# One bank and one copy for the convolution's last rows, and the second up unit's weight sums ahead of its operand sums

## The chip, the cores and the metric

The kernel runs on one core of a Trainium2 chip. The metric is the device time of one execution in microseconds (us). The text uses the profile's names for the engines: PE is TensorE, DVE is VectorE, ACT is ScalarE, SP is the engine whose queue issues the DMAs. The program holds a list of instructions for each engine, and an engine goes through its list in order.

## What the kernel computes

One step of an encoder with one layer runs over 1024 prompt frames and 64 sample frames of width 1024 (T = 1088 columns). Two parts matter here. The first is the convolution module, whose last 30 inputs of either group are outputs of their own:

```python
u = a * jax.nn.sigmoid(g)
ext = jnp.concatenate([hist, u], axis=1)          # 30 rows of history, then the frames
y = depthwise_conv(ext, w, width=31) + bias       # 256 channels
yn = layer_norm(y) * ln_g + ln_b
return jax.nn.silu(yn), ext[:, -30:]              # conv output, and conv_p or conv_s
```

The second is the MLP at the end, `x + square(relu(rmsnorm(x) @ w_up)) @ w_down`, with 4096 hidden columns. Between them lie three attention mixers, the output projection `w_out` and an attention over 256 memory tokens.

## The kernel before

All big products are made of single-precision numbers split into a high and a low part (`split`, lines 168 to 171): ACT writes the high part, DVE subtracts it from the source and writes the low part. A product then takes three matmuls, high by high, high by low and low by high.

**What sets the order.** The order on each engine is made when the program is built. A planner plays the program through on a clock of its own, and gives each engine, whenever it is free, the ready instruction with the lowest priority number. The number counts up with the program text (`tc.cur_priority`); the text adds to it or sets it in a few places. A tile of a pool has a fixed number of buffers for each tag, and an instruction that first writes a tile can run only when a buffer of that tag is free.

**The mixer stage.** Four lanes (projections, attention, convolution, HGRN) are written as generators and interleaved; each has its own range of numbers, in the order projections, attention, HGRN, convolution, then the matmuls of the projections, and last everything behind the mixers (`PR_END`). The convolution (`lane_conv`, lines 758 to 836) works in three pieces of the time axis; both halves of the 256 channels (`ct`) have a tile `ext` of inputs and a tile `y` of sums. The 31 taps are 62 instructions on DVE for a piece (lines 788 to 794), a chain for each `ct`. In the last piece they are followed in the text by the last 30 columns: two transposes on PE into a PSUM tile `pco`, a copy by DVE into `cvo` (line 804) and a DMA, first for the prompt, then for the sample. PSUM tag `cv` has one buffer, so the second pair of transposes waits for the first copy. After them come the means and variances (`pme`, `pva`), the normalization, and the DMA of the result into `mix_d`. `cvo` takes its buffer from tag `c0` (one buffer, also used by `sg` and `rs`); tag `nat` of pool `wk` (two buffers) holds transposed keys and values on their way out, last those of the memory (`mnat`, line 402).

**The first products behind the mixers.** `dense_add(0, w_out, ...)` (line 1104) multiplies `w_out` by the mixers' outputs of the first 512 columns; its matmuls write `pa`. For each block of weights the low part `wl` is made by DVE.

**The up projection.** The hidden columns are made in 16 units of 256 (line 1367). Unit 0 is a plain product. Units 1 to 15 are Strassen-like: seven products of half size instead of eight. For this the operand is turned once into sums (`forms`, line 1302): for each of four `k`, `T1` and `T2` and `T3` and `T4` are made in place from the normalized columns and then split. The names of the operands are `B11`, `T1`, `B21`, `T2`, `B22`, `T3`, `T4`. For each unit the weights are turned into sums too (`sums`, lines 1328 to 1333, four additions of 128x512 that write into the loaded tiles `r1` and `r2`), and split into `S2`, `S1`, `S3`, `S4`, `A22`. The products of unit 1 come in the order `W` (first half of `pa` by `B11`), `W` (second half by `B21`, after ACT has copied the first result), `Y = S4 B22`, `Z = S2 T2`, `X = S1 T1`, then into the same PSUM tile `Z` again `S3 T3` and `A22 T4`, each time after DVE has added what was there to an output tile (`plus`, line 1344). Both weight tiles of a unit (`pa`, `pb`) come from tags `wh` and `wl`, which have two buffers; unit 1 gets them when unit 0 has used its own (`ws`). The second group's columns are normalized by `second` (line 1291), which runs 600 numbers late beside the end of the product before.

Of the kernel before, what the change touches and what calls it, by code (L numbers as in the profile page):

```python
# [8 lines left out]
F32 = mybir.dt.float32  # L9
# [8 lines left out]
P = 128  # L18
# [6 lines left out]
G = 256  # L25
# [27 lines left out]
def kernel(ctx: ExitStack, tc: tile.TileContext, *args):  # L53
    nc = tc.nc
# [18 lines left out]
    def act(out, in_, func, **kw):  # L73
        nc.scalar.activation(out=out, in_=in_, func=func, **kw)  # L74

    V, Q = nc.vector, nc.gpsimd
# [4 lines left out]
    ident = const.tile([P, P], F32, name="ident")  # L81
# [28 lines left out]
    for m in LEVELS[1:]:  # L110
        nb = 64 // m
        f = const.tile([P, nb], F32, name=f"lf{m}", tag="lvlf", bufs=1)
# [56 lines left out]
    def split(hi, lo, src):  # L169
        act(hi, src, AF.Copy)  # L170
        V.tensor_tensor(out=lo, in0=src, in1=hi.bitcast(F32), op=ALU.subtract)  # L171
# [5 lines left out]
    def fetch_w(src, r0, kt, c0, cols=P):  # L177
        raw = wp.tile([P, KD, P], F32, name="wr", tag="wr")[:, :kt, :cols]
        nc.sync.dma_start(out=raw, in_=src[r0:r0 + kt * P, c0:c0 + cols].rearrange("(k p) c -> p k c", p=P))
        return raw  # L180
# [43 lines left out]
    def pair(which):  # L224
        return [pools[which].tile([P, 576], F32R, name="ap", tag="ap") for _ in range(2)]
# [16 lines left out]
    wk = mx.enter_context(tc.tile_pool(name="wk", bufs=2))  # L242
    rb = wk.tile([P, T], F32, name="rb", tag="rb", bufs=1)
    with ExitStack() as pa:
# [6 lines left out]
        for i, (t0, n) in enumerate(TT):  # L251
# [3 lines left out]
            if i in (3, 6):  # L255
                c = (C_SK, C_SV)[i // 3 - 1]
# [43 lines left out]
    ps_cv = mx.enter_context(tc.tile_pool(name="ps_cv", bufs=1, space=PSUM))  # L300
# [169 lines left out]
    def halves(t):  # L470
        return t[:, :PAST], t[:, PAST:]
# [266 lines left out]
    HW = CW - 1  # L738
    CN = 376
    CE = SP - 2 * CN + HW + SS  # L740

    def ct_(name, tag, n=CN):
        return hc.tile([P, n], F32, name=name, tag=tag)
# [6 lines left out]
    ps = ps_cv.tile([P, 4, 64], F32, name="pcw", tag="cv")  # L750
# [7 lines left out]
    def lane_conv():  # L758
        tails = [None, None]
        for t0, np_ in ((0, CN), (CN, CN), (2 * CN, SP - 2 * CN)):  # L760
            last = t0 + np_ == SP
            n, nt = (CE, np_ + SS) if last else (np_, np_)
            ys, exts = [], []
# [32 lines left out]
                if j % 3 == 2:  # L796
                    yield 0.3 + n / 150.0
            if last:
                for at, dst in ((np_, conv_p), (CE, conv_s)):
                    ps = ps_cv.tile([P, G], F32, name="pco", tag="cv")  # L800
                    for ct in range(2):
                        nc.tensor.transpose(ps[:HW, ct * P:(ct + 1) * P], exts[ct][:, at:at + HW], ident)
                    ot = ct_("cvo", "c0")
                    V.tensor_copy(out=ot[:HW, :G], in_=ps[:HW])
                    nc.sync.dma_start(out=dst[0, 0], in_=ot[:HW, :G])
            rs = ct_("rs", "c0").rearrange("p (j n) -> p j n", j=2)
            sqs = [ct_(f"sq{ct}", f"ce{ct}", CN + HW) for ct in range(2)]
            for p0, pn in ((0, n // 2), (n // 2, n - n // 2)):
# [197 lines left out]
    class Lane:  # L1006
# [3 lines left out]
        def ready(self):  # L1010
            return self.need is None or self.need in done

    lanes = [Lane(lane_projections(), P_COST, PR_PROJ), Lane(lane_attention(), 1.0, PR_ATT),
             Lane(lane_conv(), 1.0, PR_CONV), Lane(lane_hgrn(), 1.0, PR_HGRN)]
    while lanes:
        ln = min((x for x in lanes if x.ready()), key=lambda x: x.t)
# [38 lines left out]
    def unit(tag, dt=F32):  # L1055
        return units[tag].tile([P, 576], dt, name=tag, tag=tag)

    xw = [[unit("xt") for k in range(KD)] for g in range(2)]
# [202 lines left out]
    def bank():  # L1261
        return psm.tile([P, 512], F32, name="pw", tag="w", bufs=2)

    def banks():
        return psm.tile([P, 2, 512], F32, name="pz", tag="z", bufs=3)
# [4 lines left out]
    def mul(ps, w, b, start, cols):  # L1270

        for k, (bh, bl) in enumerate(b):
            last = k == len(b) - 1
            mm(ps, w[0][:, k], bh[:, cols], start and k == 0, False, skip_group_check=not start)
            mm(ps, w[0][:, k], bl[:, cols], False, False, skip_group_check=not start)
            mm(ps, w[1][:, k], bh[:, cols], False, last, skip_group_check=not start)

    def mul2(ps, w, b, start, n=N2):
        mul(ps[:, 0, :HN], w, b, start, slice(0, HN))
        mul(ps[:, 1, :n - HN], w, b, start, slice(HN, n))  # L1280
# [21 lines left out]
    def forms(k):  # L1302

        (h11, h12), (h21, h22) = ((xw[0][i], xw[1][i]) for i in (k, k + 4))
        V.tensor_tensor(out=h11[:, :N1], in0=h12[:, :N1], in1=h11[:, :N1], op=ALU.subtract)
        act(h11[:, N1:], h12[:, N1:], AF.Copy)
        split(*hb[T1][k], h11)
        V.tensor_tensor(out=h12, in0=h22, in1=h12, op=ALU.subtract)
        V.tensor_tensor(out=h22, in0=h22, in1=h11, op=ALU.subtract)
        split(*hb[T2][k], h22)  # L1310
        split(*hb[T3][k], h12)
        V.tensor_tensor(out=h21[:, :N1], in0=h21[:, :N1], in1=h22[:, :N1], op=ALU.subtract)
        split(hb[T4][k][0][:, :N1], hb[T4][k][1][:, :N1], h21[:, :N1])
# [9 lines left out]
    def wform(src):  # L1323
        pr = [unit("ap", F32R)[:, :4 * P].rearrange("p (k c) -> p k c", k=4) for _ in range(2)]
        split(*pr, src)
        return pr

    def sums(a11, a12, a21, a22, s1, eng):

        eng.tensor_tensor(out=s1, in0=a21, in1=a22, op=ALU.add)  # L1330
        eng.tensor_tensor(out=a21, in0=a11, in1=a21, op=ALU.subtract)
        eng.tensor_tensor(out=a11, in0=s1, in1=a11, op=ALU.subtract)
        eng.tensor_tensor(out=a12, in0=a12, in1=a11, op=ALU.subtract)

    def square(out, c, scale=None):

        if scale is None:
            act(out, c, AF.Relu)
        else:
            V.scalar_tensor_tensor(out=out, in0=c, scalar=0.0, in1=scale, op0=ALU.max, op1=ALU.mult)  # L1340
        act(out, out, AF.Square)

    def plus(out, a, b, eng=V):
        eng.tensor_tensor(out=out, in0=a, in1=b, op=ALU.add)  # L1344

    def store_hidden(i, tiles):
        for m, g, t in zip((0, 0, 1, 1), (0, 1, 0, 1), tiles):
            t0, n, _ = GR[g]
            nc.sync.dma_start(out=hid_d[2 * i + m][:, t0:t0 + n], in_=t[:, :n])
# [17 lines left out]
    for i in range(1, NU):  # L1367
        r1 = fetch_w(w_up, 0, KD, 2 * i * P)
        r2 = fetch_w(w_up, 0, KD, (2 * i + 1) * P)
        pa, pb = ([wp.tile([P, KD, P], F32R, name=nm, tag=nm) for nm in ("wh", "wl")] for _ in range(2))  # L1370
        split(*pa, r1)
        if i == 1:
            tc.cur_priority += 800
            for k in range(4):
                forms(k)
        s1 = fz.tile([P, 4, P], F32, name="s1", tag="s1", bufs=1)
        sums(r1[:, :4], r1[:, 4:], r2[:, :4], r2[:, 4:], s1, V)
        S2, S1 = wform(r1[:, :4]), wform(s1)
        S3 = wform(r2[:, :4])
        S4, A22 = [t[:, :4] for t in pb], [t[:, 4:] for t in pb]  # L1380
        split(*S4, r1[:, 4:])
        split(*A22, r2[:, 4:])
        t1 = t1s[i % 2]
        W, Z, X = bank(), banks(), banks()
        mul(W, [t[:, :4] for t in pa], hb[B11], True, slice(0, N1))
        act(t1[:, :N1], W, AF.Copy)
        c12, c22 = unit("ap"), unit("ap")
        if i == 1:

            mul(W, [t[:, 4:] for t in pa], hb[B21], False, slice(0, N1))  # L1390
            Y = banks()
            mul2(Y, S4, hb[B22], True)
            plus(halves(c12), halves(t1), Y[:, :, :HN])
        mul2(Z, S2, hb[T2], True)
        plus(halves(c12), halves(c12 if i == 1 else t1), Z[:, :, :HN])
        mul2(X, S1, hb[T1], True)
        plus(halves(c22), halves(t1), X[:, :, :HN])
        if i == 1:
            plus(halves(c12), halves(c12), X[:, :, :HN])
        else:  # L1400
            mul(W, [t[:, 4:] for t in pa], hb[B21], False, slice(0, N1))
        c11 = unit("xt")
        square(c11[:, :N1], W)
        mul2(Z, S3, hb[T3], False)
        plus(halves(c22), halves(c22), Z[:, :, :HN])
        square(c22, c22, q)
        if i > 1:
            mul2(X, S4, hb[B22], False)
            plus(halves(c12), halves(c12), X[:, :, :HN])
        square(c12, c12, q)  # L1410
        mul2(Z, A22, hb[T4], False, N1)
        c21 = unit("xt")
        plus(c21[:, :HN], t1[:, :HN], Z[:, 0, :HN])
        plus(c21[:, HN:N1], t1[:, HN:N1], Z[:, 1, :N1 - HN])
        square(c21[:, :N1], c21[:, :N1])
        store_hidden(i, (c11, c12, c21, c22))
# [63 lines left out]
    for c in range(NC):  # L1480
# [5 lines left out]
        if c < NC - 1:  # L1486
            for j in range(KD // 2):
                for m, w in enumerate(down_w(c, j, None)):
                    ps = bank()
                    mul(ps, w, [hid[k][0] for k in range(NF)], True, slice(0, N1))  # L1490
                    plus(xT[0][2 * j + m], xT[0][2 * j + m], ps)
                    ps = banks()
# [3 lines left out]
        else:  # L1496

            ws = []
            for j in range(KD // 2):
                dst = [[t[:, :NF * P].rearrange("p (k c) -> p k c", k=NF) for t in pair(1 - c % 2)] for m in range(2)]  # L1500
                ws += down_w(c, j, dst)
            for g, c0, n in ((0, 0, 512), (1, 0, 320), (1, 320, 256)):
                for m in range(KD):
                    ps = bank()[:, :n]
# [37 lines left out]
```

## Time and profile before

| | before |
|---|---|
| median of 3 runs | 1772.66 us (1772.01 to 1775.33) |
| the profiled execution | 1772.62 us, span 1770.6 us |
| PE busy | 1698.2 us, 96% of the span |
| DVE busy | 1174.6 us, 66% |
| ACT busy | 791.5 us, 45% |
| granted TensorE clock, mean | 0.987 |

The span runs from the first to the last instruction; 2.0 us of the execution lie around it. A clock of 1.00 is the level of 2.4 GHz and 0.50 that of 1.2 GHz. Successive DVE instructions overlap by some 0.09 us at their ends, so that one listed with 0.69 us takes 0.60 us of the engine's time from start to start.

### The profile page before, as it was taken

To read this page: it belongs to the slowest core of one execution; us is meant where nothing else is said; L and a number is where in the kernel's file an instruction comes from. 1 tells how busy PE (TensorE), PEld (TensorE's weight loads), DVE (VectorE), ACT (ScalarE), POOL (GpSimd) and SP (SyncE) were. 2 spreads that over 40 slices of the span, in tenths; PEclk is the share of its full clock that TensorE was granted. 3 is DMA by queue.
4 is the path that set the end of the run, shared out by engine and by line. 5 is a ranking of instruction groups with operands and counts; after the bars stand their busy time and mean duration, and the time that the engine had idled before them with its cause. 6 is when DMAs were issued, how large, how long until landed. Compare 5 with 4: busy or idle time off the path is not lost.

```text
span 1770.6 us, 29390 instructions
## 1 busy us (share of the span) xinstructions
PE 1698.2 (96%) x11379; PEld 1506.6 (85%) x11379; DVE 1174.6 (66%) x2231; ACT 791.5 (45%) x1614; POOL 93.6 (5%) x201
## 2 busy tenths in 40 slices
PE   6999999999999979999999989999999999999997
PEld 4987768788777768988899979999999999999987
DVE  6366789988986897668777795555555444444435
ACT  5266657647356755346456353343334212122213
POOL 3021201101020100000000000000000000000000
PEclk9999999999999989999999999999999999999999
DMA  8521322243237357222522323333335732332112
GB/s 255 144 76 44 111 78 84 80 113 88 63 99 215 101 155 233 81 88 68 158 78 72 118 91 107 99 99 103 101 100 194 272 98 87 98 99 73 36 36 102
DMA packets 233195, 194.70 MB, mean 110 GB/s; under 512 B 17502, under 2 KB 199711, under 8 KB 233055
## 3 DMA queue, kind: packets, MB, share of 16 engines
q1 hardware_dynamic: 232799, 192.80, 35.5%
q8 instruction: 90, 1.47, 0.4%
q14 instruction: 50, 0.41, 0.1%
q0 software_dynamic: 256, 0.01, 0.0%
HBM read 137.96 MB, written 53.72 MB: 108 GB/s over the span
## 4 chain that ended last, share of the span: by engine, by line
PE 78%; DVE 13%; ACT 4%; DMA 2%; issue 2%; POOL 0%; SPq 0%; DVEq 0%; POOLq 0%; ACTq 0%
PE pz L71 25%; PE pw L71 16%; PE pm L71 11%; PE pa L71 9%; PE pq L71 5%; PE z L71 2%; DVE y L794 2%; PE pmo L71 2%; PE pms L71 1%; PE po L71 1%; PE pt L517 1%; PE pv L71 1%; DVE hsc L933 1%; DVE sba L494 1%; DVE wl L171 1%
## 5 line engine op out<-in xcount | busy, mean ns | idle before, releaser
L74 ACT ACTIVATE wh<-wr 128x1024 fp32r<-128x1024 f32 (+1 forms) x179 | 161.5, 910 | 446.6 <-PE pz L71 193.8
L171 DVE TENSOR_TENSOR wl<-wr,wh 128x1024 fp32r<-128x1024 f32 (+1 forms) x179 | 184.5, 1037 | 68.8 <-ACT wh L74 67.6
L71 PE MATMUL pw<-ap,wh 128*128 128x512 f32 x720 | 223.4, 391 | 1.3 <-ACT t L74 0.7
L71 PE MATMUL pz<-ap,wh 128*128 128x288 f32 x988 | 198.3, 294 | 0.0
L71 PE MATMUL pa<-ap,wh 128*128 128x256 f32 (+2 forms) x768 | 187.1, 332 | 2.2 <-DVE xt L1119 2.2
L71 PE MATMUL pm<-hx,wh 128*128 128x512 f32 (+1 forms) x640 | 176.4, 364 | 1.9 <-ACT wh L74 1.7
L71 PEld LDWEIGHTS pz<-ap,wh 128*128 128x128 f32 x988 | 161.3, 188 | 4.7
L71 PE MATMUL pm<-ap,wh 128*128 128x256 f32 (+1 forms) x768 | 164.7, 308 | 0.0
L71 PEld LDWEIGHTS pw<-ap,wh 128*128 128x128 f32 x720 | 130.1, 188 | 24.1 <-ACT t L74 1.1
L71 PE MATMUL pz<-ap,wl 128*128 128x288 f32 x494 | 145.5, 294 | 0.0
L71 PEld LDWEIGHTS pa<-ap,wh 128*128 128x128 f32 x768 | 131.7, 190 | 12.6 <-DVE xt L1119 2.4
L71 PE MATMUL pw<-ap,wl 128*128 128x512 f32 x360 | 140.4, 390 | 0.0
L71 PE MATMUL pa<-ap,wl 128*128 128x512 f32 (+2 forms) x384 | 126.8, 331 | 1.1 <-DVE wl L171 1.1
L71 PEld LDWEIGHTS pm<-hx,wh 128*128 128x128 f32 x640 | 110.5, 192 | 20.3 <-ACT wh L74 2.5
L71 PEld LDWEIGHTS pm<-ap,wh 128*128 128x128 f32 x768 | 123.9, 191 | 4.2 <-issue 1.7
L1344 DVE TENSOR_TENSOR xt<-xt,pz 128x576 f32<-128x576 f32 x56 | 42.2, 754 | 113.8 <-PE pz L71 108.5
L71 PE MATMUL pm<-ap,wl 128*128 128x256 f32 (+1 forms) x384 | 114.2, 297 | 0.0
L71 PE MATMUL pm<-hx,wl 128*128 128x512 f32 (+1 forms) x320 | 112.9, 353 | 0.3 <-DVE wl L171 0.2
L794 DVE SCALAR_TENSOR_TENSOR y<-ext,cwT,y 128x376 f32<-128x376 f32 (+1 forms) x180 | 101.1, 609 | 0.3
L1344 DVE TENSOR_TENSOR xt<-xt,pw 128x512 f32<-128x512 f32 (+2 forms) x80 | 51.1, 639 | 69.6 <-PE pw L71 69.6
L71 PE MATMUL pq<-ap,wh 128*128 128x512 f32 (+2 forms) x384 | 93.1, 332 | 0.0
L71 PEld LDWEIGHTS pz<-ap,wl 128*128 128x128 f32 x494 | 92.7, 188 | 0.0
(380 smaller groups left out, 3580.7 us busy)
## 6 DMA issues: line engine op xcount, KB each, us to landing
wr<-in_w_up_dram SPq DMA_DIRECT2D x32, 512.0 KB, 4.0
wr<-in_w_down_dram SPq DMA_DIRECT2D x32, 512.0 KB, 3.5
wr<-in_w_in_dram SPq DMA_DIRECT2D x24, 512.0 KB, 4.3
hid_d<-ap SPq DMA_DIRECT2D x32, 288.0 KB, 2.5
aq<-hid_d SPq DMA_DIRECT2D x32, 288.0 KB, 3.2
wr<-in_w_out_dram SPq DMA_DIRECT2D x16, 512.0 KB, 3.5
wr<-in_w_mq_dram SPq DMA_DIRECT2D x16, 512.0 KB, 3.7
wr<-in_w_mo_dram SPq DMA_DIRECT2D x32, 256.0 KB, 2.7
```

Of the source, the lines that this page charges most:

```text
L71: nc.tensor.matmul(out, lhsT=lhsT, rhs=rhs, start=start, stop=stop, **kw)
L74: nc.scalar.activation(out=out, in_=in_, func=func, **kw)
L171: V.tensor_tensor(out=lo, in0=src, in1=hi.bitcast(F32), op=ALU.subtract)
L494: V.tensor_tensor_scan(out=v[:, ::-1], data0=z[:, n - 1:0:-1], data1=v[:, ::-1], initial=-NEG, op0=ALU.add, op1=ALU.subtract)
L517: nc.tensor.transpose(ps[:w, j - jb], p[:, j * P:j * P + w], ident)
L794: V.scalar_tensor_tensor(out=y, in0=ext[:, j:j + n], scalar=cwT[:, ct, j:j + 1], in1=y, op0=ALU.mult, op1=ALU.add)
L933: V.copy_predicated(sc[r, s_at:s_at + ng, :, r].rearrange("p g h (c w) -> p (g h) c w", w=2 * m)[:, :, :, m:], lvl[m][r, par * nb:(par + 1 ...
L1344: eng.tensor_tensor(out=out, in0=a, in1=b, op=ALU.add)
```

## The change

The last rows of the convolution, prompt and sample, are transposed into one PSUM tile of a bank; one copy takes both out into a buffer of tag `nat`, and two DMAs store the halves. `forms` is cut in two: `forms` makes `T1` and `T2`, and a new `forms2` makes `T3` and `T4`; the text of unit 1 now first has the weight sums and their splits and then the operand sums, `T1` and `T2` of all four `k` ahead of `T3` and `T4`. The 800 numbers that were added in front of the operand sums are still added in front of them, so that the weight sums of unit 1 no longer have them.

```diff
             if last:
-                for at, dst in ((np_, conv_p), (CE, conv_s)):
-                    ps = ps_cv.tile([P, G], F32, name="pco", tag="cv")
+                ps = ps_cv.tile([P, 2, G], F32, name="pco", tag="cv")
+                for o, at in enumerate((np_, CE)):
                     for ct in range(2):
-                        nc.tensor.transpose(ps[:HW, ct * P:(ct + 1) * P], exts[ct][:, at:at + HW], ident)
-                    ot = ct_("cvo", "c0")
-                    V.tensor_copy(out=ot[:HW, :G], in_=ps[:HW])
-                    nc.sync.dma_start(out=dst[0, 0], in_=ot[:HW, :G])
+                        nc.tensor.transpose(ps[:HW, o, ct * P:(ct + 1) * P], exts[ct][:, at:at + HW], ident)
+                ot = wk.tile([P, 512], F32, name="cvo", tag="nat").rearrange("p (o c) -> p o c", o=2)
+                V.tensor_copy(out=ot[:HW], in_=ps[:HW])
+                for o, dst in enumerate((conv_p, conv_s)):
+                    nc.sync.dma_start(out=dst[0, 0], in_=ot[:HW, o])
...
         split(*hb[T2][k], h22)
+
+    def forms2(k):
+
+        (h11, h12), (h21, h22) = ((xw[0][i], xw[1][i]) for i in (k, k + 4))
         split(*hb[T3][k], h12)
         V.tensor_tensor(out=h21[:, :N1], in0=h21[:, :N1], in1=h22[:, :N1], op=ALU.subtract)
         split(hb[T4][k][0][:, :N1], hb[T4][k][1][:, :N1], h21[:, :N1])
...
         split(*pa, r1)
-        if i == 1:
-            tc.cur_priority += 800
-            for k in range(4):
-                forms(k)
         s1 = fz.tile([P, 4, P], F32, name="s1", tag="s1", bufs=1)
         sums(r1[:, :4], r1[:, 4:], r2[:, :4], r2[:, 4:], s1, V)
...
         split(*A22, r2[:, 4:])
+        if i == 1:
+            tc.cur_priority += 800
+            for f in (forms, forms2):
+                for k in range(4):
+                    f(k)
```

## Rows read from the trace of the kernel before

**Rows 1.** The page: busy us (share of the span) xinstructions
```profile
PE 1698.2 (96%) x11379; PEld 1506.6 (85%) x11379; DVE 1174.6 (66%) x2231; ACT 791.5 (45%) x1614; POOL 93.6 (5%) x201
```
**Rows 2.** Waits of PE, 640 to 1100 us: total, times, longest
```profile
PE pco L802 <- DVE cvo L804: 8.6, 1, 8.6
PE pz L71 <- ACT wh L74: 5.8, 1, 5.8
...
PE pw L71 <- ACT t L74: 0.7, 1, 0.7
```
**Rows 3.** Stretches: length, busy PE PEld DVE ACT POOL, PEclk, DMA, GB/s
```profile
657.40:662.00 4.60, 4.58 (x12) 3.91 (x13) 3.23 (x5) 0.68 (x1) 0.00 (x0) 0.50 0.69 199
...
1058.30:1062.10 3.80, 3.74 (x14) 3.39 (x15) 1.70 (x3) 0.48 (x1) 0.00 (x0) 0.50 0.31 85
...
1026.80:1060.00 33.20, 26.68 (x153) 23.39 (x153) 33.09 (x55) 20.84 (x36) 0.00 (x0) 0.93 0.14 51
```
**Rows 4.** Timeline of PE, 595 to 662 us: start, us, what, [idle]
```profile
609.32 0.28 PE L802 MATMUL pco<-ident,ext 128*30 128x128 f32 x1
...
645.86 1.20 PE L71 MATMUL pa<-ap,wh 128*128 128x512 f32 x4
655.68 0.61 PE L802 MATMUL pco<-ident,ext 128*30 128x128 f32 x2 [8.62 <-DVE cvo L804]
657.42 0.80 PE L71 MATMUL pa<-ap,wl 128*128 128x512 f32 x1 [1.12 <-DVE wl L171]
```
**Rows 5.** Timeline of DVE, 643 to 660 us
```profile
644.01 11.32 DVE L794 SCALAR_TENSOR_TENSOR y<-ext,cwT,y 128x366 f32<-128x366 f32 x22
655.23 0.40 DVE L804 COPY cvo<-pco 30x256 f32<-30x256 f32 x1
655.56 0.67 DVE L171 TENSOR_TENSOR ap<-mix,ap 128x512 fp32r<-128x512 f32 x1
656.16 1.21 DVE L171 TENSOR_TENSOR wl<-wr,wh 128x1024 fp32r<-128x1024 f32 x1
```
**Rows 6.** Groups of instructions by form, DVE, the whole span
```profile
L310 DVE COPY aT<-pt 128x512 f32<-128x512 f32 x11 | 7.5, 686 | 0.2 <-PE pt L517 0.2
```
**Rows 7.** The chain that ended last: start, us, what
```profile
660.77 1.22 PE pme L71 x4
...
1033.63 12.47 PE pz L71 x94
...
1109.20 9.27 PE pz L71 x72
...
1121.25 6.36 PE pz L71 x48
```
**Rows 8.** Timeline of SP, 540 to 660 us: DMAs of `mnat`
```profile
613.83 0.45 SPq L402 DMA_DIRECT2D out_dram<-mnat  x1
...
644.55 0.39 SPq L402 DMA_DIRECT2D out_dram<-mnat  x1
```
**Rows 9.** Timeline of PE, 1051 to 1064 us
```profile
1052.14 0.39 PE L71 MATMUL pw<-ap,wl 128*128 128x512 f32 x1
1058.31 0.85 PE L71 MATMUL pz<-fz,wh 128*128 128x288 f32 x2 [5.78 <-ACT wh L74]
```
**Rows 10.** Timeline of DVE, 1005 to 1100 us
```profile
1040.91 1.22 DVE L171 TENSOR_TENSOR wl<-wr,wh 128x1024 fp32r<-128x1024 f32 x1
...
1051.29 0.68 DVE L1330 TENSOR_TENSOR s<-wr 128x512 f32<-128x512 f32 x1
...
1056.90 0.69 DVE L1333 TENSOR_TENSOR wr<-wr 128x512 f32<-128x512 f32 x1
...
1059.31 0.69 DVE L171 TENSOR_TENSOR ap<-wr,ap 128x512 fp32r<-128x512 f32 x1
1063.96 0.75 DVE L1344 TENSOR_TENSOR ap<-t,pz 128x576 f32<-128x576 f32 x1 [3.96 <-PE pz L71]
```
**Rows 11.** Timeline of ACT, 1038 to 1066 us
```profile
1039.62 1.06 ACT L74 ACTIVATE wh<-wr 128x1024 fp32r<-128x1024 f32 x1 [0.50 <-PE pz L71]
```

## The prediction

> **What bounds the kernel now.** The page's first part comes first: PE is busy for 96% of the span [rows 1], so little but PE's idle time and the stretches at its lower clock can be won. The view of waits, for PE alone, says where that idle time lies behind the mixers: one wait of 8.6 us in front of the transposes `pco`, one of 5.8 us in front of a product `pz`, and small ones, as 0.7 us at `pw` [rows 2]. The table of stretches shows what each of the two long waits leaves behind it: a stretch in which PE is busy throughout but at 0.50, the level of 1.2 GHz (657.4 to 662.0 and 1058.3 to 1062.1 us, [rows 3]). Both waits are what the two edits touch. Last come the timelines of PE and DVE around the waits, to see who is late, and who is late next.
>
> **Edit 1, the convolution's last rows.** In PE's list the second pair of transposes stands behind the first four `pa` products; those end at 647.1, the pair starts at 655.68 and waits for the first `cvo` copy [rows 4]. The first pair ran long before (609.32, [rows 4]). With one tile for all four, none needs a copy first, and I expect the second pair beside the first one. The wait at `pco` goes. What is late next stands two rows on: the next `pa` product waits for `wl` until 657.42 [rows 4], and DVE makes `wl` only behind 22 taps in a row, the copy and a low part `ap` [rows 5]. Nothing in the edit takes these off DVE, and the taps have lower numbers than all that follows the mixers. So PE idles nearly as long as before. Term by term:
> - The copy on this path now takes 512 columns for 256. Copies cost 0.40 us for 30x256 [rows 5] and 0.69 for 128x512 [rows 6]: `wl` is 0.29 us later, +0.3. The second copy, which goes, ran behind this `wl`, beside a busy PE: nothing.
> - The mean's four products `pme` need the last tap and the bank behind the copy. Before they ran in the middle of the `pa` products and cost the chain 1.22 us [rows 7]. Now they can run at 656, while PE waits for `wl`: -1.2, if the planner puts them ahead; 0 if not. I take -1.2, since their numbers are lower than those of `pa`.
> - Two transposes more at 597 to 610, 0.3 us each by [rows 4], in a list that meets the wait above anyway: 0; exposed they cost +0.6.
> - The stretch at 0.50 begins with the idle time and I keep it whole; if PE's work starts 1.4 us sooner, up to -0.7 (half of that).
>
> Sum of edit 1: -0.9 us. Its ends: +0.9 (both doubtful ones lost) and -1.9.
>
> **Edit 2, the second up unit.** Between 1026.8 and 1060.0 us DVE has no idle time (33.09 of 33.20 us, [rows 3]): it makes the operand sums and, last of all, the four weight sums and their splits, from 1051.29 to 1060.0 [rows 10]. PE starts the last product of `W` at 1052.14 [rows 9], is free at 1052.4 and needs `S4`, which needs all four sums; the fourth starts at 1056.90 [rows 10], and PE starts at 1058.31 [rows 9]. The work on DVE is the same after the change (9 instructions of 0.60 us from start to start, 5.4 us, go to the front); only its order changes. So I date each product by what DVE has finished when PE comes for it.
> - The third sum writes over `r1`, which the split of `pa` reads. That split starts on ACT at 1039.62 behind a PE product, as `wh` comes free [rows 11], and ends on DVE at 1042.1 [rows 10]. Sums three and four then end at 1043.3, `S2`, `S1`, `S3` at 1045.1. `S4` and `A22` need the second `wh` buffer, which unit 0 leaves with its last product at 1046.1 [rows 7]; with two results of unit 0 in between I put `S4` at 1047.5. PE wants it at 1052.4, so the wait of 5.8 us is gone.
> - PE then takes 3.18 us each for `Y`, `Z`, `X` and `S3 T3` (6.36 for two) and 2.91 for `A22 T4` (9.27 less twice 3.18, [rows 7]): `Z` starts at 1055.6, `X` at 1058.8, `S3 T3` at 1061.9, `A22 T4` at 1065.1, end at 1068.0.
> - `T3` and `T4` are eight instructions of 0.60 us and four of 0.66 (0.75 less the 0.09 by which DVE's instructions overlap, [rows 10]), 7.5 us; as they are last now, `T1` and `T2` are done by 1060.0 - 7.5 = 1052.5. `Z` has 3 us to spare, `T4` 5 us.
> - New on the path: `S3 T3` goes into the PSUM tile of `Z`, and must wait for two `plus` on DVE (`Y`, then `Z`), 0.66 us each, which have higher numbers than `forms2`. They end at 1060.0 + 1.3 = 1061.3, 0.6 us before PE comes. Before, the first of them ran at 1063.96 [rows 10]. This is the thinnest cover in the sum: each microsecond that DVE loses beyond 0.6 is a microsecond of PE's.
> - The wait gone, the stretch at 0.50 behind it goes: 3.74 us of work at half the clock are 1.87 at the full one [rows 3], -1.9.
> - The weights of unit 2 are loaded when `r1` and `r2` are read for the last time, at about 1048 and no longer at 1059, and are early. In `A22 T4`'s wait for its own `plus` PE has `W` of unit 2, as before; without it +0.7.
> - The 0.7 us for which `W` waits for ACT [rows 2] I leave; `Y`, now ready, could fill it: -0.7.
>
> Sum of edit 2: -5.8 - 1.9 = -7.7 us, ends -8.4 and, with DVE late by 4 us, -3.7. Behind unit 1 the chain is PE alone (two runs of `pz` of 9.27 and 6.36 us in a unit, with `pw` between them, [rows 7]), so nothing gives the gain back.
>
> **The sum** is made against the profiled execution, 1772.62 us (span 1770.6 and 2.0 around it), which is the median of the runs, 1772.66, within 0.04: 1772.6 - 0.9 - 7.7 = 1764.0 us.
>
> **Rivals.**
> - A, *the wait moves to the `plus`*. For it: the 0.6 us above, and a DVE list without any slack. Against it: DVE lost nothing to waits in this stretch before. If DVE comes 4 us late, PE waits some 3.5 at `S3 T3`: 1767.5.
> - B, *the sums block DVE's list*, the slower one. Sums one and two can run at 1027; if the planner, on its own clock, puts the split of `pa` and the third sum right behind them, DVE stands from 1028 until 1040.9, when ACT has written `wh`: h = 12.9 us, with all operand sums behind it. The `plus` then end at 1074.2, `S3 T3` is 12.3 late, and the clock falls again (+1.9 back): 1772.6 - 0.9 - 7.7 + 12.3 + 1.9 = 1778.2. It decides from h = 7.3 us on (0.6 to spare and 8.6 - 1.9 to lose). Against it: the list before stood nowhere for that split, though its number was as low then.
> - The Trainium skill bears on B ("TensorE: Matmul & The Clock Gate", Part 1, Engine queue depths): it says that VectorE's queue is strictly first in, first out, so a sum waiting at the head would hold everything behind it. By it B costs what stands above, and if ready ones could pass a waiting one the time would be the forecast's; no run here shows it, as DVE had no wait in that stretch.
> - C, *`nat` is short*. The copy's buffer is one of two that the memory's rows also use: 6 more `mnat` tiles go out from 613.83 to 644.55 [rows 8]. If the copy's tile took its buffer with the transposes and the others queued behind it, six products of 12 matmuls of 256 columns would slip behind the taps, 1.8 us each (half of the 0.30 us of a `pa` product of 512 columns, [rows 4], twelve times): 1764.0 + 10.8 = 1774.8 at worst, 1769.4 with half. Against it: the buffer is only taken when the copy runs, at 655.
> - D, *edit 2 does not do what it says*: the planner finds the sums not ready as long as `pa` waits for `wh`, fills DVE with operand sums, and `S4` still comes late; what is left is edit 1 and 1 or 2 us: 1770.5.
>
> **How the numbers follow.** Forecast 0.60, A 0.16, D 0.08, C 0.08, B 0.08. What a measurement of this kernel can tell from no change is about 0.2%, 3.5 us: faster is below 1769.1. The forecast (its own range 1762.5 to 1767) is all faster; of A 0.13 and of C 0.03. Same: A 0.03, D 0.08, C 0.05, B 0.01. Slower: B 0.07. Together 0.76, 0.17, 0.07. The range, 1760 to 1771.5, starts below the sum's lower end (1772.6 - 1.9 - 8.4 = 1762.3), since a new order of the list from 597 us on can also win something, and takes in A, D and half of C; B and the rest are left out.
>
> **What would show it.** Right: no wait of PE at `pco`, one of about 9 us at `wl`; the stretch behind it still at 0.50; `pme` before the long run of `pa`; PE without a wait and at 1.00 from 1049 to 1068; the last sum on DVE near 1043; unit 2 about 8.6 us earlier. Wrong: a `pz` that waits for DVE's `plus` (A), a DVE wait for ACT's `wh` or a load around 1030 (B), `mnat` copies behind 650 (C), the fourth sum still behind 1050 (D). A PE that starts on `wl` well before 657 would show that the taps do not hold it, and edit 1 would be mis-sized by up to its 8.6 us.

## The result, and the profile after

| | before | after |
|---|---|---|
| median | 1772.34 us (4 runs) | 1841.80 us (4 runs, 1840.37 to 1843.38) |
| ratio, 95% interval | | 1.0388 [1.037, 1.0406] |
| span of the profiled execution | 1770.6 us | 1839.5 us |
| mean granted clock | 0.987 | 0.963 |

The change costs 69 us. The forecast was a gain of 8.6. One of the ten executions of a kernel below (the turn half way through the memory) took 2365.98 us at a granted clock of 0.653; it is in the median given there and in no ratio.

The page says first where. Its first part and two lines of its second, which cut the span into 40 slices of 46 us:

```profile
PE 1716.8 (93%) x11366; PEld 1516.2 (82%) x11379; DVE 1176.6 (64%) x2230; ACT 793.0 (43%) x1614; POOL 100.1 (5%) x201
...
PE   6999999999745699999999999999999999999997
...
PEclk9999999999955799999999999999999999999999
```

The work is that of [rows 1], apart from some 19 us of PE time, which matmuls at the lower clock take more. But PE has a hole from 460 to 640 us (slices 11 to 14), and its clock falls in it. The hole lies ahead of both edits' places in time: the transposes were expected at 610 and 655, the sums behind 1020. The table of stretches gives its size. Kernel before, then after (length; busy PE, PEld, DVE, ACT, POOL with their instructions, where PEld is PE's loading of weights; PEclk, DMA share, GB/s):

```profile
500.00:650.00 150.00, 136.54 (x1122) 114.52 (x1120) 124.14 (x276) 102.59 (x253) 22.41 (x34) 0.96 0.47 136
```

```profile
500.00:650.00 150.00, 84.26 (x466) 60.37 (x465) 103.09 (x253) 48.87 (x143) 25.44 (x34) 0.61 0.20 53
```

In these 150 us PE runs 656 matmuls fewer. Nearly half of them (312) are the projections' own. The same view, restricted to their tile `pm`, says when they are missing (columns PE, PEld, DVE, ACT; before, then after):

```profile
480.00:520.00 40.00, 28.24 (x156) 23.33 (x156) 3.18 (x6) 0.00 (x0) 1.00 0.36 106
520.00:560.00 40.00, 22.33 (x132) 19.55 (x132) 0.92 (x2) 1.53 (x4) 0.87 0.61 169
560.00:600.00 40.00, 16.77 (x120) 15.01 (x120) 0.00 (x0) 1.86 (x5) 1.00 0.50 145
600.00:640.00 40.00, 20.04 (x144) 17.97 (x144) 0.00 (x0) 2.27 (x6) 1.00 0.46 134
```

```profile
480.00:520.00 40.00, 6.42 (x42) 5.47 (x40) 0.91 (x2) 0.00 (x0) 0.71 0.20 57
520.00:560.00 40.00, 0.00 (x0) 0.00 (x0) 0.00 (x0) 0.00 (x0) 0.50 0.16 47
560.00:600.00 40.00, 5.49 (x12) 3.80 (x12) 0.00 (x0) 0.00 (x0) 0.54 0.06 17
600.00:640.00 40.00, 24.25 (x132) 20.86 (x132) 3.20 (x6) 0.00 (x0) 0.84 0.26 79
```

The projections stand still from 491 to 587 us. The timelines of after show what held them; PE, ACT and DVE (start, us, what, and in brackets the idle time of the engine and who ended it):

```profile
480.50 0.60 PE L365 MATMUL pn<-ident,kT 128*128 128x128 f32 x4
491.92 0.38 PE L365 MATMUL pn<-ident,kT 128*128 128x128 f32 x2
...
586.85 1.22 PE L71 MATMUL pm<-hx,wh 128*128 128x512 f32 x2 [2.33 <-ACT nat L74]
...
593.78 0.55 PE L365 MATMUL pn<-ident,kT 128*128 128x128 f32 x3 [1.44 <-ACT nat L74]
```

```profile
586.22 0.58 ACT L74 ACTIVATE nat<-pn 128x512 f32<-128x512 f32 x1
593.34 0.38 ACT L74 ACTIVATE nat<-pn 128x256 f32<-128x256 f32 x1 [6.54 <-DMA out_dram<-nat]
610.43 0.38 ACT L74 ACTIVATE nat<-pn 128x256 f32<-128x256 f32 x1 [16.70 <-DMA out_dram<-cvo]
```

```profile
607.75 0.67 DVE L804 COPY cvo<-pco 30x512 f32<-30x512 f32 x1
```

The keys of the last attention pair are transposed into two banks (`pn`) at 480.5 and 491.9, and copied out into tiles of tag `nat` only at 586.2 and 593.3. In the kernel before, ACT makes the same three copies as soon as the transposes are done:

```profile
478.60 0.60 ACT L74 ACTIVATE nat<-pn 128x512 f32<-128x512 f32 x1 [2.39 <-PE pn L365]
486.30 0.38 ACT L74 ACTIVATE nat<-pn 128x256 f32<-128x256 f32 x1 [1.15 <-PE pn L365]
492.90 0.38 ACT L74 ACTIVATE nat<-pn 128x256 f32<-128x256 f32 x1 [1.72 <-PE pn L365]
```

The projections' banks (`pm` and `pn` share a tag of two) are full till 586, so the next `pm` waits for the `nat` copy. The third copy waits 16.7 us for the DMA of `cvo`. The first has no wait of its own: it stands that late in ACT's list, where the planner put it.

The reason that the experiments bear out is in the program text. The lanes are interleaved in it, and there the convolution's tail comes ahead of the last three `nat` tiles and all sixteen `mnat`. The planner gives a tag's buffers to its tiles in the order of the text, and `cvo` is written only behind the last tap. Everything of that tag further down in the text queues behind the convolution, and behind that queue stand the projections of the last pair and of the memory.

The second edit is in the same execution. Unit 0's first product `pw` starts 77.4 us later than before (1098.48 for 1021.08), the last instruction 68.9 us later; so 8.5 us are won in between. DVE's list around it (the first, the fourth sum, and the low part of `S4`), and two stretches:

```profile
1104.30 0.69 DVE L1335 TENSOR_TENSOR s<-wr 128x512 f32<-128x512 f32 x1 [0.64 <-DMA wr<-in_w_up_dram]
...
1122.69 0.68 DVE L1338 TENSOR_TENSOR wr<-wr 128x512 f32<-128x512 f32 x1
...
1124.56 0.68 DVE L171 TENSOR_TENSOR wl<-wr,wh 128x512 fp32r<-128x512 f32 x1
```

```profile
1126.20:1145.40 19.20, 19.16 (x128) 17.77 (x127) 19.20 (x30) 9.85 (x17) 0.00 (x0) 1.00 0.33 100
1104.20:1137.40 33.20, 33.20 (x212) 30.78 (x212) 33.10 (x55) 21.28 (x37) 0.00 (x0) 1.00 0.24 75
```

The second of them is the stretch of 33.2 us of [rows 3], 77.4 us on: PE ran 26.68 us of it then, now all of it, at 1.00.

### The profile page after: what moved, and what is told of

It reads as the page before. It is cut to its first block, busy times and chain, and to the rows that moved or that the text cites. A ratio compares the mean times of both kernels' runs of the same rounds, so it can differ in the third digit from the quotient of the medians.

```text
span 1839.5 us, 29412 instructions
## 1 busy us (share of the span) xinstructions
PE 1716.8 (93%) x11366; PEld 1516.2 (82%) x11379; DVE 1176.6 (64%) x2230; ACT 793.0 (43%) x1614; POOL 100.1 (5%) x201
## 4 chain that ended last, share of the span: by engine, by line
PE 76%; DVE 12%; DMA 4%; ACT 4%; issue 2%; POOL 1%; SPq 0%; DVEq 0%; POOLq 0%; ACTq 0%
PE pz L71 24%; PE pw L71 16%; PE pm L71 11%; PE pa L71 9%; PE pq L71 5%; DVE y L794 2%; PE z L71 2%; PE pmo L71 1%; PE pms L71 1%; PE po L71 1%; PE pt L517 1%; DVE hsc L934 1%; DVE sba L494 1%; PE pv L71 1%; DMA wr<-in_w_mk_dram 1%
```

## Experiments

Ratios are to the kernel before on the same chip, with 95% intervals; its median was 1773.6 to 1774.6 us there. Theory 1 is the one above: the tile's turn in the text. The rivals are that the bank (or edit 2) does it, or that the tag has too few buffers, whatever the order.

**Edit 2 alone** (the convolution's tail as before; the diff is that of the change from its first `...` on).

```diff
-        if i == 1:
-            tc.cur_priority += 800
...
         split(*A22, r2[:, 4:])
+        if i == 1:
+            tc.cur_priority += 800
...
```

> Only the second edit (weight sums ahead, operand sums in two parts); the convolution's rows as before. If the whole loss lies in the first edit, and the second did what the sum said, the time is 1772.6 - 8.5 = 1764.1 us (8.5 is the difference between the shift of unit 0, +77.4 us, and that of the end, +68.9 us, in the changed kernel). If the second edit shares in the loss, the time is above 1772.

1764.24 us, ratio 0.9951 [0.9935, 0.9966]. Edit 2 is worth what was forecast for it; the loss is all edit 1's.

**Only the tag of the copy's tile**, still two banks and two copies.

```diff
-                    ot = ct_("cvo", "c0")
+                    ot = wk.tile([P, 512], F32, name="cvo", tag="nat")
```

> The kernel before with one change: both copies of the convolution's last rows go into buffers of tag nat; two PSUM tiles and two copies as before. Theory 1 (the buffers of a tag are given out in the order of the text, so that the projections' nat tiles behind the copy in the text wait for the taps): about 1850 us (1772.6 + 77), or more as two tiles now stand in front of them. Theory 2 (the bank shared by all four transposes, held from them to the copy, reorders the lanes): 1772 us, no change.

1853.43 us, ratio 1.045 [1.0421, 1.0478]. This one line makes the whole loss. Two `cvo` now take both buffers, and ACT's wait for them grows from 16.7 us (total, times, longest), with the same hole in PE:

```profile
ACT nat L74 <- DMA out_dram<-cvo: 23.4, 1, 23.4
```

```profile
500.00:650.00 150.00, 78.22 (x442) 55.92 (x443) 102.97 (x254) 48.40 (x142) 25.50 (x34) 0.60 0.17 49
```

**Only the bank**: four transposes into one tile, two copies into `c0`.

```diff
+                ps = ps_cv.tile([P, 2, G], F32, name="pco", tag="cv")
...
+                for o, dst in enumerate((conv_p, conv_s)):
                     ot = ct_("cvo", "c0")
+                    V.tensor_copy(out=ot[:HW, :G], in_=ps[:HW, o])
```

> The kernel before with one change: all four transposes into one PSUM tile, but two copies into tag c0 as before, no nat. Theory 1: no loss; PE's 8.6 us at pco go, but PE then waits for wl at 657.4 us, so 1772.6 us within 1 us. If that wait were not covered by wl: 1764. Theory 2: about 1850 us.

1774.94 us, ratio 1.0004 [0.9995, 1.0014]: no loss, and no gain. The wait at `pco` is gone, and PE waits for the next thing on DVE's list, as long as before; the stretch behind it keeps its low clock:

```profile
647.10 1.20 PE L71 MATMUL pa<-ap,wh 128*128 128x512 f32 x4
658.81 0.80 PE L71 MATMUL pa<-ap,wl 128*128 128x512 f32 x1 [10.51 <-DVE wl L171]
```

```profile
658.80:663.40 4.60, 4.59 (x11) 3.49 (x12) 4.12 (x8) 1.19 (x3) 0.00 (x0) 0.50 0.58 168
```

**The whole change, the tail's text behind the memory's.**

```diff
+        done.add("kv text")          # end of memory_kv
...
             if last:
+                yield Need("kv text")
```

> The whole change, with one bank, one copy and tag nat, but the convolution's lane goes on in the text only when the memory's keys and values have been written down, so that the copy's tile comes behind all other nat tiles in the text. Theory 1: the loss is gone, and both edits give what was forecast, 1772.6 - 0.9 - 8.5 = 1763.2 us. If it is the tag's two buffers, whatever the order of the text: 1841 us, as the change.

1764.85 us, ratio 0.9951 [0.9935, 0.9968]. The tile, tag, bank and copy are those of the changed kernel; only the turn differs, and the loss is gone. So theory 1 is shown from both sides: the tag with the early turn makes the loss, and the turn alone takes it away. PE's timeline has the order that the prediction gave edit 1, with `pme` in the idle time:

```profile
645.42 1.20 PE L71 MATMUL pa<-ap,wh 128*128 128x512 f32 x4
655.66 1.59 PE L71 MATMUL pme<-y,ones 128*128 128x183 f32 x4 [9.04 <-DVE cvo L806]
657.40 0.80 PE L71 MATMUL pa<-ap,wl 128*128 128x512 f32 x1
```

**How much each tile behind the copy costs.** Two turns between these ends: behind the three key tiles but ahead of the memory, and half way through the memory.

```diff
+                yield Need(("fox", 1))          # e9
...
+                if m == 0 and src is w_mv: done.add("kv text")     # e10, at a middle block
+                yield Need("kv text")
```

> The whole change, but the conv tail's text comes after that of the last attention projection: the copy's tile takes its turn among the nat buffers behind the three fox1 key tiles and the first mnat, ahead of 15 of the 16 mnat. This tells which of the tiles behind the copy carry the loss. Theory 1a (the memory's own tiles carry it: while mnat waits for the copy, its transposes hold a projection bank, and the memory's projections stand still behind it): most of the loss stays, 1805 to 1835 us. Theory 1b (the three key tiles of fox1 carry it, since the last attention pair waits for what stands behind them; the mnat cost what the prediction's rival C priced, some 1.8 us each for six of them): 1764 to 1776 us.

> The same with the turn in the middle of the memory: behind nine mnat, ahead of seven. Theory 1a in proportion to the projections that stand behind the copy (7 of 16 of the 77 us at most): 1770 to 1800 us. Theory 1b: 1764 to 1768 us, as when the turn is behind all.

1800.38 us, ratio 1.0154 [1.0135, 1.0172], and 1778.07 us, ratio 1.0025 [1.0015, 1.0035]. By the text, all sixteen `mnat` stand behind the copy in the first and eight in the second, one more than each expectation counted. In the trace two of them go out shortly ahead of the copy in either kernel, through the tag's other buffer. In both, one `mnat` waits 11.0 us for the copy's DMA, and the projections stop: in 560 to 600 us with the earlier turn, behind 600 with the later one, where the kernel before has 144 matmuls of `pm` in 600 to 640. The wait and the `pm` stretch of the first, then a `pm` stretch of the second:

```profile
ACT mnat L74 <- DMA out_dram<-cvo: 11.0, 1, 11.0
```

```profile
560.00:600.00 40.00, 0.00 (x0) 0.00 (x0) 0.00 (x0) 0.00 (x0) 0.87 0.13 37
```

```profile
600.00:640.00 40.00, 5.06 (x36) 4.49 (x36) 0.00 (x0) 0.77 (x2) 0.88 0.27 81
```

The first of them also shows that the order holds the tiles, and not a full tag. Its last key tile leaves at 494.4 us, and the convolution's copy comes at 640.1. The first `mnat` is transposed between them, and is copied out some 81 us later without a wait of its own. In the planner's order it stands right behind the convolution's copy, ahead of which it had no turn; on the chip the copy itself runs later.

```profile
546.47 0.38 PE L399 MATMUL pn<-ident,mkvT 128*128 128x128 f32 x2
628.01 0.38 ACT L74 ACTIVATE mnat<-pn 128x256 f32<-128x256 f32 x1
```

From the ratios, over 0.9951 with none behind and times 1773 us: eight `mnat` behind cost 13 us, sixteen 36, sixteen and three key tiles 77. Each ratio is uncertain by 2 to 3 us. Neither expected theory had it alone: the memory's tiles cost 1.6 us each (the last eight) to 2.9 (the eight ahead of them, 23 us), the three key tiles 41 us together.

**Which half of edit 2.** First the sums in front with `forms` undivided, then the division in the old place.

```diff
+            for k in range(4):               # e5, behind the weight sums
+                forms(k); forms2(k)
...
+            for f in (forms, forms2):        # e6, ahead of the weight sums
+                for k in range(4): f(k)
```

> The kernel before with one half of edit 2 alone: the second up unit's weight sums and splits stand ahead of the operand sums, but forms is not divided (each k is done whole, its T3 and T4 operands included, before the next k). Conv tail as before. Theory (the place of the sums is what counts: TensorE waited for the weight forms S2, S1, which stood behind the operand sums on VectorE and ScalarE): the whole 8.5 us of edit 2 stay, 1764 to 1766 us. Rival (the division is what counts, because three k of T3 and T4 work, about 2.1 us of VectorE each by 0.75 + 0.68 + 0.68, stand ahead of the last T2 operand): up to 6.3 us of it is lost, 1769 to 1772 us.

> The kernel before with the other half of edit 2 alone: forms is divided into T1, T2 first and T3, T4 behind, but both still stand ahead of the weight sums. Conv tail as before. Theory (the place of the sums counts): the sums are as late as before, 1771 to 1774 us, no change. Rival (the division counts): 1764 to 1767 us.

1767.30 us, ratio 0.9958 [0.9945, 0.9971], and 1773.61 us, ratio 0.9998 [0.9986, 1.0011]. The place of the sums is the gain; the division adds nothing that the intervals tell from zero. PE's waits around unit 1 say the same: with the sums in front the largest is 0.9 us, with the division alone the old one is there:

```profile
PE pw L71 <- DVE wl L171: 0.9, 1, 0.9
```

```profile
PE pz L71 <- ACT wh L74: 6.0, 1, 6.0
```

**Is PE's idle time at the mixers' end worth anything?** Two ways to shrink it, each with two banks (on edit 2 alone) and with one (on the kernel whose turn is behind the memory): the first operands of `w_out` ahead of the last taps, and the last chunk's loads and gate ahead of everything.

```diff
+    tc.cur_priority = PR_CONV - 10 ** 5       # e7, e8: first block of w_out, splits of its operands
...
+                if last: tc.cur_priority = PR_PROJ - 10 ** 5     # e11, e12: loads, sigmoid, gating
```

> Edit 2 alone, and the operands of the output projection's first block (its weight split and the eight splits of the mixed rows of the first 512 tokens) are given a place ahead of the last convolution taps on the engines' lists; conv tail in two banks with two copies as before. Theory (the end of the mixer is set by VectorE's list, in which the first wl stands behind 22 taps, so TensorE is idle some 9 us whatever the bank does): the first block's 24 matmuls, of which 4 ran ahead already, fill that gap: 20 x 0.217 = 4.3 us, and up to 1.9 us more by the clock: 1764.2 less 4 to 6 = 1758 to 1760 us. Rival (VectorE itself is the bound here, so that work moved ahead of the taps only delays the taps): no change, 1764 us.

> The same early operands of the output projection, on the whole change with the copy's tile taking its turn behind the memory keys and values (the kernel of e4_later_in_text). With the cover gone (TensorE no longer waits for VectorE's list behind the taps), what the one bank is worth shows as the difference from e7_early_out_weights: theory 1 (in both kernels the rows' statistics come behind the first block's matmuls, so that the second pair of transposes is no bound) says 0 to 1.5 us better than it, 1757 to 1760 us; the rival (the one bank removes a wait of 8.6 us, hidden till now) says 5 to 8 us better than it, 1751 to 1755 us.

> Edit 2 alone, with the prologue of the convolution's last chunk (its loads, sigmoid and gating) placed ahead on the lists; two banks and two copies as before. In the kernel before the loads of this chunk are issued at 562.84 and its gating multiply comes at 596.2, while VectorE idles some 8 of 25 us at 550 to 575: the 62 taps start late and end the mixer. Theory (TensorE's idle 9 us at 646 to 657 come from taps that start too late): taps start some 20 us earlier, fewer of them stand in one block behind the last projection, and TensorE's gap shrinks: 1764.2 less 3 to 9 = 1755 to 1761 us. Rival (VectorE's list is as full whatever comes first, or the scheduler fills the gap with something else): 1764 us, no change.

> The same early prologue on the whole change with the turn behind the memory (the kernel of e4_later_in_text). Theory: as e11_early_conv_two_banks, 1755 to 1761 us; what the one bank is worth then is the difference between the two. By the rule that the second pair's wait is covered only as long as the taps end last: 0 to 3 us better than two banks; the rival (one bank and two differ in nothing that the end waits for): within 1 us.

| | two banks | one bank |
|---|---|---|
| as it was | 1764.24, 0.9951 | 1764.85, 0.9951 |
| early `w_out` operands | 1763.91, 0.9941 [0.9919, 0.9963] | 1762.76, 0.9941 [0.992, 0.9962] |
| early conv loads | 1766.58, 0.9951 [0.9937, 0.9966] | 1766.48, 0.9955 [0.994, 0.997] |

The gap did shrink. With edit 2 alone PE waits 8.6 us at `pco`; with the early operands, then with the early loads:

```profile
659.30 0.61 PE L802 MATMUL pco<-ident,ext 128*30 128x128 f32 x2 [4.80 <-DVE cvo L804]
```

```profile
656.74 0.39 PE L806 MATMUL pco<-ident,ext 128*30 128x128 f32 x2 [1.41 <-DVE cvo L808]
```

The time did not follow: 4 to 6 us and 3 to 9 us were expected, 1.8 us at most and 0 were measured, with intervals that overlap those of the kernels they were made from. One bank or two makes no difference in any row that the intervals could show. DVE is busy for all of 650 to 660 in the three kernels of two banks, and what was moved ahead pushed other work of its list behind it: with the early operands 27 taps stand in the last block for 22 (13.86 us for 11.31), with the early loads attention and HGRN instructions run among the taps till 656. That DVE's total work bounds this stage fits, but it was not tested by taking work off DVE. The fastest kernels measured are those with early `w_out` operands, 1762.8 and 1763.9 us; they beat both kernels of this case, but not each other nor edit 2 alone by a margin that the intervals separate.

## Why the prediction was wrong, and where it was right

**The step that failed** is the sentence that set rival C aside: "the buffer is only taken when the copy runs, at 655". The copy does run that late in its stage (607.75 in after). But the text gives the turn, and it holds for the tiles behind: they get no buffer until the copy has had its own. So C's count was wrong. The prediction counted the six `mnat` that go out after the first transposes by the clock of the trace [rows 8]; what queues are the tiles that come later in the text, whatever the clock: three key tiles and sixteen `mnat`. C's price was misread too: a projection of the memory is 24 matmuls of 256 columns (384 for the sixteen, in the trace before) and not 12, which at the prediction's own rate makes 3.6 us a tile and not 1.8. Measured were 1.6 to 2.9 for an `mnat`; that 1.8 lies there is luck, and a key tile cost some 14. So 10.8 us "at worst" became 36 and, with the keys, 77. And the first sign was at hand: the section on the order, ahead of the prediction, says that a first write needs a free buffer, and the text of the lanes says who asks first.

A part of the 77 us may be the clock, which the prediction gave C no term for. In 500 to 600 us PE was at 0.52 in after and busy for 48.16 of 100 us. All of PE's work took some 19 us more than before, so the clock's part can't be much over that. How much of the loss is the wait and how much the lower clock of what ran in it, no run separates.

**Edit 1, point by point** (by the kernels that do not have the turn). The wait at `pco` goes, and the next is as long and on DVE: right (10.51 for `wl` in the bank alone; 9.04 with the whole change, where `pme` meets it first). `pme` ahead of the `pa` products: right with one copy, not with two. The clock's stretch stays: right in the bank alone, 0.50; with the whole change it is shorter, 0.78 over 657.4 to 662.0. The sum of -0.9 us (whose lower end should read -1.6, as its +0.3 was not in doubt) is below what the runs can tell: the bank alone came out between -0.9 and +2.5 us (0.9995 to 1.0014), and with edit 2 it changed nothing that shows (0.9951 in both).

**Edit 2**: -7.7 was forecast, -8.5 measured in the trace and -8.7 by the ratio of edit 2 alone (0.0049 of 1773, interval -6.0 to -11.5). The dates that PE meets hold when after's are moved back by 77.4 us: `wl` of `S4` ends at 1047.8 (forecast 1047.5), the product `S3 T3` starts at 1061.8 (1061.9). The fourth sum, ahead of them, ends at 1046.0 and not at 1043.3, which cost nothing. The wait of 5.8 us and the stretch at 0.50 are gone. So is the 0.7 us wait of `W`, filled by `Y`, which the prediction had left as a possible -0.7: -5.8 - 1.9 - 0.7 = -8.4 is the trace's 8.5 within 0.1.

The thinnest cover, the two `plus`, was used up. DVE's line is the second of them; PE was free 0.6 us before its end, put two matmuls of unit 2's `W` there, and began `S3 T3` 0.06 us behind it:

```profile
1138.40 0.74 DVE L1349 TENSOR_TENSOR ap<-ap,pz 128x576 f32<-128x576 f32 x1
1138.54 0.62 PE L71 MATMUL pw<-ap,wh 128*128 128x512 f32 x2
1139.20 0.66 PE L71 MATMUL pz<-ap 128*128 128x288 f32 x3
```

So A came as far as its condition and cost nothing, as PE had other work. B's mark, a wait of DVE for a load, is there with 0.64 us of the 7.3 from which B decides. D did not come. (In the sum, A's 4 us of delay are priced once as 3.5 and once, in the end of -3.7, as 4; the first agrees with its own cover of 0.6.)

**The marks** that the prediction set were the right ones: "`mnat` copies behind 650 (C)". In after they run from 649.1 to 730.9 us. Only the chance of 0.08 and the size rested on a step that could have been settled from the text.

## What to carry to other kernels

Before a tile is put into an existing pool tag, list every tile of that tag in the order of the program text and compare it with the order in time: a late writer that stands early in the text stops all that follow it, and whatever they hold. Move the text (as in the kernel of 1764.85 us) or keep another tag (as with the bank alone, 1774.94), and then look at the time. A wait of an engine that is busy for 96% of the span is worth its length only where nothing else stands right behind it: 5.8 us at `pz`, with the slow stretch and a short wait beside it, gave 8.5 us, and 8.6 us at `pco` gave none.

## What the runs showed that was not expected

- One buffer, wanted for a copy of 0.67 us, kept two PSUM banks full for 94 us (491.92 to 586.22). The convolution's turn held up the projections' copies, and the full banks their next products; PE ran 656 matmuls fewer in 500 to 650 us.
- A PE that is starved also ran slower here: in 520 to 560 us it was busy for 18.18 us at a granted clock of 0.50, where it was busy for 35.06 at 0.87 before.
- The length of the idle time in front of `pco` could be set to 8.6, 4.8 or 1.4 us, and the kernel's time stayed within 0.1% (0.9951, 0.9941, 0.9951).
